# Low-rank projections ahead of the recurrence, and gemms cut in thirds, in an RWKV-7 and band-attention trunk

## The chip, the cores and the metric

The kernel runs on one core of a Trainium2 chip. The metric is the time of one execution in microseconds of device time, as the median of three runs. The engines are TensorE (PE, with its weight loads PEld), VectorE (DVE), ScalarE (ACT), GpSimd (POOL) and SyncE (SP), which issues most of the DMAs.

## The reference

One step of an encoder with a layer of RWKV-7 time mixing and a layer of chunk-band attention, each followed by a SwiGLU network, for a prompt of 1024 tokens and eight samples of 16 tokens; the width is 1024 in 16 heads of 64. The part that the change touches is the time mixing:

```python
def wkv7_scan(r, w, k, v, a, b, s0):
    def step(s, inp):
        r_t, w_t, k_t, v_t, a_t, b_t = inp
        sa = jnp.einsum('bhij,bhj->bhi', s, a_t)
        s = s * w_t[:, :, None, :] + sa[..., None] * b_t[:, :, None, :] + v_t[..., None] * k_t[:, :, None, :]
        y = jnp.einsum('bhij,bhj->bhi', s, r_t)
        return s, y
...
    r = xr @ w_r
    w_log = -jax.nn.softplus(-(w0 + jnp.tanh(xw @ w1) @ w2)) - 0.5
    decay = jnp.exp(-jnp.exp(w_log.astype(jnp.float32)))
    k = xk @ w_k
    v = xv @ w_v
    a_gate = jax.nn.sigmoid(a0 + (xa @ a1) @ a2)
    g = jax.nn.sigmoid(xg @ g1) @ g2
    kk = l2_normalize(to_heads(k * k_k, H_A))
    k = k * (1.0 + (a_gate - 1.0) * k_a)
    y, wkv_new = wkv7_scan(rh, to_heads(decay, H_A), kh, vh, -kk, kk * to_heads(a_gate, H_A), wkv_prev)
    # each head of y is normalised, scaled by ln_w, ln_b, a bonus of r, k and v is added
    out = (y * g) @ w_o
```

xr, xw, xk, xv, xa and xg are mixtures of each token's row and the row before it. The state s runs through the whole prompt; each sample has a state of its own.

## The kernel before

All tokens, 1024 of the prompt and 128 of the samples, lie in three blocks of 384. Every block goes through `proj(b)`, which computes what the recurrence reads and stores it to DRAM, in this order:

- the low-rank stage `proj_lora` (decay, gate a and output gate g), in seven steps: three inner products, two of `gates`, two of `outputs`;
- the key gemms `proj_k`, eight, one a step, each with a long tail of small operations on ScalarE and VectorE;
- the receptance gemms `proj_r`, eight, one a step, taking turns with `inverses(b)`, which forms the product of `kk` and `b` for each window (tiles `pa`, `G`, `Aab`), solves 16x16 triangles on VectorE and merges them to 64x64 inverses `TT` (tiles `t11`, `p1`);
- `proj_h` of the next block (norm and modulation), then the value gemms `proj_v`, eight, one a step.

A gemm is 24 matmuls of 128x384 into a bank `acc`: eight pieces along the width, three matmuls each, because weights and inputs are split into a high and a low part.

The recurrence is computed in windows of 128 tokens, w = 0 to 8, three a block; windows 0 to 7 are the prompt, 8 the samples. Each window has two halves of the heads, hf = 0 and 1, which run side by side. `win_prep` loads the window (tiles `XL`, `BK`, `UV`) and forms its products in banks `G`; `win_state` takes two chunks of 64 tokens, each in three steps (X, U, D, in banks `st`, two of them), and carries the state `S`; `win_y` makes the output in bank `Y`; `win_post` copies it to `y` (L1028), normalises it with two matmuls, `cen` and `var`, in banks `st`, and stores it as `yg` (L1043). A window of a block reads the values of that block, so the windows of block b run beside the projections of block b + 1:

```python
for _ in self.alternate(w, self.proj(b), 5, 4):
```

Five steps of the windows, then four of the projections, until both are done. The windows of the third block come last, in the order (6,0) (6,1) (8,0) (7,0) (7,1) (8,1), five steps to two of `early()`: first the rest of the adaLN matmuls (bank `aux`, weights `raw<-in_wada`), then the output projections of blocks 1 and 2. The third block's output projection follows when all windows are done; it reloads `yg` into tiles `mr` and splits them into `mx`.

The order in which steps are written is not the order on the engines. The framework's scheduler lays every instruction on its engine at build time, by the written order and by what it takes to be ready; each engine then runs its list in order. So the place of an instruction is read from the built program.

Of the kernel before, what the change touches and what calls it, by code (L numbers as in the profile page):

```python
# [16 lines left out]
NB = 3  # L17
TB = 384
KF = 8
KAPPA = float(np.exp(-0.5))  # L20


# [119 lines left out]
class Trunk:  # L142
# [120 lines left out]
    def gemm(self, out, W, hi, lo, m=128):  # L263

        whi, wlo = W
        for k in range(8):
            s = slice(k * m, (k + 1) * m)
            self.mm3(out, whi[:, s], wlo[:, s], hi[k], lo[k], k == 0, k == 7)


    def sq_open(self):
        return Ctx()
# [250 lines left out]
    def proj_r(self, b, hi, lo):  # L523

        nc = self.nc
        for f in range(8):
            W = self.wunit(self.pp, self.a["rw_r"][f])
            pz = self.bank("acc", 2)
            self.gemm(pz[:, :TB], W, hi, lo)
            kp = self.ev("ag", 2)  # L530
            self.load(kp, "kp", b, f)
            ex = self.ev("rr", 2)
            self.load(ex, "cs", b, f)
            nc.scalar.activation(ex, ex, AF.Exp, scale=-KAPPA)
            nc.vector.scalar_tensor_tensor(kp, pz[:, :TB], self.P("rk", f), kp, ALU.mult, ALU.mult)
            nc.vector.tensor_tensor(ex, ex, pz[:, :TB], ALU.mult)
            self.spill("r", b, f, ex)
            aux = self.bank("aux", 1)
            mm(nc, aux[:, :TB], self.C("bo"), kp, True, True)
            bn = self.ev("e0", 3)  # L540
            nc.scalar.activation(bn, aux[:, :TB], AF.Copy)
            self.save("bn", b, f, bn)
            yield
# [94 lines left out]
    def proj_v(self, b, hi, lo):  # L638

        nc = self.nc  # L640
        for f in range(8):
            W = self.wunit(self.pp, self.a["rw_v"][f])
            pz = self.bank("acc", 2)
            self.gemm(pz[:, :TB], W, hi, lo)
            if b in (2,):
                self.step(1)
            vv = self.ev("vv", 2)
            self.load(vv, "bn", b, f)
            v = self.ev("e0", 3)
            nc.scalar.activation(v, pz[:, :TB], AF.Copy)  # L650
            nc.vector.tensor_tensor(vv, vv, pz[:, :TB], ALU.mult)
            nc.scalar.activation(vv, vv, AF.Identity, bias=self.P("lnb", f))
            self.spill("v", b, f, vv)
            pt = self.bank("aux", 1)
            for w in range(3):
                nc.tensor.transpose(pt[:, w * 128:(w + 1) * 128], v[:, w * 128:(w + 1) * 128], self.C("ident"))
            vt = self.ev("e0", 3)
            nc.scalar.activation(vt, pt[:, :TB], AF.Copy)
            for e in range(2):
                nc.sync.dma_start(self.sv[b][:, :, e, f, :].rearrange("w p d -> p w d"),  # L660
                                  vt.rearrange("p (w e d) -> p e w d", w=3, e=2)[:, e])
            yield
# [7 lines left out]
    def proj_k(self, b, hi, lo):  # L670
# [3 lines left out]
        for f in range(8):  # L674
            W = self.wunit(self.pp, self.a["rw_k"][f])
            pz = self.bank("acc", 2)
            self.gemm(pz[:, :TB], W, hi, lo)
            iv = self.ev("rr", 2)
            self.load(iv, "cs", b, f)
            ag = self.ev("ag", 2)  # L680
# [337 lines left out]
    def win_post(self, w, hf, R):  # L1018

        nc = self.nc  # L1020
        b, wi = divmod(w, 3)
        fs = slice(4 * hf, 4 * hf + 4)
        gt = self.wt("gl", [128, 512], 1)
        nc.sync.dma_start(gt.rearrange("p (f t) -> p f t", f=4), self.sp[b]["g"][:, wi, fs, :])
        bv = self.wt("bv", [128, 512], 1)
        nc.sync.dma_start(bv.rearrange("p (f t) -> p f t", f=4), self.sp[b]["v"][:, wi, fs, :])
        y = self.wt("y", [128, 512], 1)
        nc.scalar.activation(y, R.Y, AF.Copy)  # L1028
        cen = self.bank("st", 2)
        mm(nc, cen, self.C("cen"), y, True, True)  # L1030
        nc.scalar.activation(y, cen, AF.Square)
        yield
        var = self.bank("st", 2)
        mm(nc, var, self.C("bo"), y, True, True)
        nc.scalar.activation(y, var, AF.Ln, bias=self.eps[:, 1:2], scale=1.0 / 64)
        nc.scalar.activation(y, y, AF.Exp, scale=-0.5)
        nc.vector.tensor_tensor(y, cen, y, ALU.mult)
        yield
        for f in range(4):
            s = slice(f * 128, (f + 1) * 128)  # L1040
            nc.vector.scalar_tensor_tensor(y[:, s], y[:, s], self.P("lnw", 4 * hf + f), bv[:, s], ALU.mult, ALU.add)
        nc.vector.tensor_tensor(y, y, gt, ALU.mult)
        nc.scalar.dma_start(self.yg[b][:, fs, wi * 128:(wi + 1) * 128], y.rearrange("p (f t) -> p f t", f=4))  # L1043
# [112 lines left out]
    def layer0a(self, ctx):  # L1156
# [4 lines left out]
        with ExitStack() as c2:  # L1161
            self.proj_open(c2)
            for _ in self.proj(0):
                pass
            for b in range(1, NB):
                w = self.windows([(w, hf) for w in range(3 * b - 3, 3 * b) for hf in range(2)])
                for _ in self.alternate(w, self.proj(b), 5, 4):
                    pass
        self.tail_open(ct)
        self.nraw, self.nhi, self.nlo = (2, 2, 2)  # L1170
# [756 lines left out]
```

## Time and profile before

| | us |
|---|---|
| median of three runs | 3878.44 (3875.95 to 3879.47) |
| profiled execution | 3879.81 |
| its span, first to last instruction | 3878.0 |
| TensorE busy | 3545.9 |
| VectorE busy | 2292.3 |
| ScalarE busy | 1570.7 |
| RWKV layer up to its last output gemm | 1334.1 |
| mean granted TensorE clock | 0.926 |

The profile is that of one execution. Busy time of TensorE is modelled from pipelined matmuls, so that a stage in which it is busy nine tenths is not yet full; the granted clock beside it says how fast it ran. A 32-bit matmul stands in the trace as two or more records, so the counts in the profile are higher than those of the program. The tables below count the program's matmuls.

### The profile page before, as it was taken

The numbers are of one execution on the slowest core, as the hardware profiler recorded it, in microseconds if no ns is written. First come the engines' busy times: TensorE is split into PE (matmuls) and PEld (weight loads), VectorE is DVE, ScalarE is ACT, GpSimd is POOL, SyncE is SP. The second block draws the span as 40 slices with busy tenths as digits, with TensorE's granted clock in tenths as the row PEclk, the third lists the DMA queues.
The fourth block names the chain that finished last, engine by engine and source line by source line (L and its number), as shares of the span: only waits on it lengthen the run. The fifth ranks groups of instructions, "written<-read, shape, count | busy, mean of one in ns | idle before, by whom it ended". The sixth has DMA issues, their size and how long they took to land.

```text
span 3878.0 us, 72281 instructions
## 1 busy us (share of the span) xinstructions
PE 3545.9 (91%) x28614; PEld 3130.7 (81%) x28614; DVE 2292.3 (59%) x4388; ACT 1570.7 (41%) x2966; POOL 570.8 (15%) x473
## 2 busy tenths in 40 slices
PE   6789889988889799999999999889889799999999
PEld 4677777867657689999887879677677799999898
DVE  4667566765435765555456842666675764555567
ACT  5555555544213533333311353465654533333310
POOL 0000000000000255444000100000000264453000
PEclk8896899798679989999999999899999899999999
DMA  5775676676646522222755113444554322222521
GB/s 205 229 237 159 182 220 170 176 219 185 185 142 194 175 71 71 75 77 77 270 192 187 68 59 100 140 141 141 150 191 162 127 79 74 74 75 92 170 84 71
DMA packets 429443, 552.31 MB, mean 142 GB/s; under 512 B 128432, under 2 KB 297520, under 8 KB 424624
## 3 DMA queue, kind: packets, MB, share of 16 engines
q1 hardware_dynamic: 374960, 528.80, 42.8%
q10 hardware_dynamic: 54144, 18.89, 2.1%
q8 instruction: 225, 3.69, 0.4%
q14 instruction: 114, 0.93, 0.1%
HBM read 413.42 MB, written 134.12 MB: 141 GB/s over the span
## 4 chain that ended last, share of the span: by engine, by line
PE 67%; DMA 11%; DVE 7%; ACT 4%; issue 2%; SPq 1%; POOL 0%; ACTq 0%; DVEq 0%; POOLq 0%
PE S L139 31%; PE PT L139 15%; PE acc L139 10%; PE st L139 3%; PE O L139 2%; PE G L139 2%; DVE h L255 1%; PE PT L1753 1%; PE Y L139 1%; PE aux L139 1%; DMA TT<-Z 1%; DMA raw<-in_wada 1%; DMA mr<-yg 1%; DMA yg<-y 1%; DMA rr<-sf_cs 1%
## 5 line engine op out<-in xcount | busy, mean ns | idle before, releaser
L139 PE MATMUL S<-h,w 128*128 128x320 f32 (+1 forms) x4944 | 696.9, 300 | 17.9 <-DVE h L255 8.3
L139 PEld LDWEIGHTS S<-h,w 128*128 128x128 f32 x4944 | 675.5, 192 | 26.0 <-DVE h L255 13.3
L139 PE MATMUL S<-h,wh 128*128 128x320 f32 (+1 forms) x2844 | 529.7, 338 | 12.7 <-DVE h L1123 6.8
L139 PE MATMUL acc<-mx,whi 128*128 128x384 f32 x1728 | 497.4, 366 | 30.3 <-ACT mx L254 12.7
L139 PEld LDWEIGHTS S<-h,wh 128*128 128x128 f32 x2844 | 455.7, 189 | 69.2 <-issue 13.3
L254 ACT ACTIVATE w<-rq 128x512 fp32r<-128x512 f32 x308 | 192.1, 629 | 502.4 <-PE S L139 199.3
L255 DVE TENSOR_TENSOR w<-rq,w 128x512 fp32r<-128x512 f32 x308 | 270.6, 882 | 199.1 <-ACT w L254 198.4
L139 PEld LDWEIGHTS acc<-mx,whi 128*128 128x128 f32 x1728 | 332.6, 201 | 60.5 <-ACT mx L254 15.6
L139 PE MATMUL PT<-h,w 128*128 128x320 f32 (+1 forms) x2448 | 355.0, 300 | 15.1 <-ACT w L254 6.9
L139 PEld LDWEIGHTS PT<-h,w 128*128 128x128 f32 x2448 | 337.4, 192 | 18.9 <-ACT w L254 7.1
L139 PE MATMUL acc<-mx,wlo 128*128 128x384 f32 x864 | 311.3, 361 | 6.6 <-DVE wlo L255 6.5
L139 PE MATMUL PT<-h,wh 128*128 128x320 f32 (+1 forms) x1428 | 287.6, 345 | 9.6 <-DVE wh L255 3.9
L1312 POOL TENSOR_TENSOR t<-t,t 128x576 f32<-128x576 f32 (+1 forms) x132 | 216.1, 1637 | 414.2 <-ACT t L1319 291.7
L139 PEld LDWEIGHTS PT<-h,wh 128*128 128x128 f32 x1428 | 234.2, 191 | 39.0 <-issue 6.9
L255 DVE TENSOR_TENSOR wlo<-raw,whi 128x1024 fp32r<-128x1024 f32 x114 | 139.9, 1230 | 96.4 <-ACT whi L254 89.3
L139 PEld LDWEIGHTS acc<-mx,wlo 128*128 128x128 f32 x864 | 172.5, 200 | 14.0 <-DVE wlo L255 9.6
L254 ACT ACTIVATE whi<-raw 128x1024 fp32r<-128x1024 f32 x114 | 119.5, 1054 | 143.0 <-PE acc L139 96.4
L255 DVE TENSOR_TENSOR h<-h,h 128x1024 fp32r<-128x1024 f32 (+4 forms) x112 | 122.9, 1112 | 84.7 <-ACT h L254 69.7
L254 ACT ACTIVATE h<-h 128x1024 fp32r<-128x1024 f32 (+4 forms) x112 | 103.2, 935 | 164.1 <-DMA h<-sd 105.3
L254 ACT ACTIVATE wh<-rq 128x512 fp32r<-128x512 f32 x124 | 74.8, 626 | 230.6 <-PE S L139 146.3
L1312 DVE TENSOR_TENSOR t<-S,t 128x576 f32<-128x576 f32 (+1 forms) x116 | 86.4, 745 | 128.5 <-PE S L139 128.5
L1379 DVE TENSOR_TENSOR h<-h,S 128x640 f32<-128x640 f32 (+1 forms) x150 | 112.1, 752 | 79.4 <-PE S L139 79.2
(423 smaller groups left out, 5712.9 us busy)
## 6 DMA issues: line engine op xcount, KB each, us to landing
h<-in_wada SPq DMA_DIRECT2D x64, 512.0 KB, 6.3
rq<-in_wg SPq DMA_DIRECT2D x88, 256.0 KB, 2.6
rq<-in_wu SPq DMA_DIRECT2D x88, 256.0 KB, 2.6
rq<-in_wd SPq DMA_DIRECT2D x88, 256.0 KB, 3.0
raw<-in_wada SPq DMA_DIRECT2D x32, 512.0 KB, 4.6
kc<-in_ck SPq DMA_DIRECT2D x16, 1024.0 KB, 5.1
vc<-in_cv SPq DMA_DIRECT2D x16, 1024.0 KB, 7.2
sd<-t SPq DMA_DIRECT2D x88, 160.0 KB, 1.9
```

What stands on the lines that cost most here:

```text
L139: return nc.tensor.matmul(out, lhsT, rhs, start=start, stop=stop)
L254: self.nc.scalar.activation(hi, x, AF.Copy)
L255: self.nc.vector.tensor_tensor(lo, x, hi, ALU.subtract)
L1312: eng.tensor_tensor(out, x, y, ALU.add)
L1379: nc.vector.tensor_tensor(y, y, d, ALU.add)
L1753: nc.tensor.transpose(pt[:, j * 128:(j + 1) * 128], P[:, j * 128:(j + 1) * 128], self.C("ident"))
```

## The change

In blocks 2 and 3 the seven low-rank steps are written ahead of the first step of the windows. Then two steps of the windows alternate with three of the projections; the key, receptance and value gemms of all blocks stop after the third and the sixth of their eight pieces, so that a gemm is three steps. The second matmul of `win_post` goes to a bank `G` in place of a bank `st`.

```diff
+LOW = 7
...
+    def gemm_steps(self, out, W, hi, lo):
+
+        whi, wlo = W
+        for k in range(8):
+            s = slice(k * 128, (k + 1) * 128)
+            self.mm3(out, whi[:, s], wlo[:, s], hi[k], lo[k], k == 0, k == 7)
+            if k in (2, 5):
+                yield
...
-            self.gemm(pz[:, :TB], W, hi, lo)
+            yield from self.gemm_steps(pz[:, :TB], W, hi, lo)
...
-        var = self.bank("st", 2)
+        var = self.bank("G", 2)
...
-                for _ in self.alternate(w, self.proj(b), 5, 4):
+                p = self.proj(b)
+                for _ in range(LOW):
+                    next(p)
+                for _ in self.alternate(w, p, 2, 3):
                     pass
```

The line with `gemm_steps` stands in `proj_k`, `proj_r` and `proj_v`.

What this does to TensorE's list is seen from its matmuls by stage. A stage runs from the first matmul of its first gemm to that of the next stage; each has 192 of its own gemms, the tail none. The tail runs from the last value gemm to the first output gemm.

| stage | before: all | windows | inverses | after: all | windows | inverses |
|---|---|---|---|---|---|---|
| block 1 low-rank | 192 | 0 | 0 | 192 | 0 | 0 |
| block 1 key | 216 | 0 | 16 | 216 | 0 | 16 |
| block 1 receptance | 247 | 0 | 48 | 247 | 0 | 48 |
| block 1 value | 439 | 0 | 224 | 439 | 0 | 224 |
| block 2 low-rank | 611 | 80 | 336 | 611 | 64 | 352 |
| block 2 key | 493 | 230 | 64 | 436 | 205 | 32 |
| block 2 receptance | 615 | 254 | 160 | 482 | 186 | 96 |
| block 2 value | 484 | 126 | 144 | 500 | 125 | 160 |
| block 3 low-rank | 611 | 96 | 320 | 577 | 158 | 224 |
| block 3 key | 471 | 223 | 48 | 479 | 88 | 192 |
| block 3 receptance | 605 | 245 | 160 | 414 | 198 | 16 |
| block 3 value | 690 | 134 | 304 | 634 | 173 | 208 |
| tail | 848 | 724 | 0 | 675 | 295 | 256 |
| output, block 1 | 371 | 179 | 0 | 470 | 278 | 0 |
| output, block 2 | 195 | 2 | 0 | 580 | 386 | 0 |
| output, block 3 | 192 | 0 | 0 | 328 | 137 | 0 |

Three places show it in the list itself. The first is TensorE in the third block's receptance stage, at the start of its third gemm (`acc_1608` before, `acc_1591` after). Before:

```order
L139 MATMUL acc_1608_9413<-mx_1346_7972,whi_1606_9409 128x384
L139 MATMUL G_1539_8944<-pa_1538_8941 64x64 x15
L139 MATMUL st_1473_8654<-xs1_1470_8632,TT_1058_6175 64x64 x8
L139 MATMUL G_1539_8944<-pa_1538_8941 64x64
L139 MATMUL Y_1545_8989<-YL_1389_8155,UV_1397_8205 64x64
L139 MATMUL G_1579_9230<-XL_1576_9220,BK_1577_9221 128x128 x3
L139 MATMUL st_1541_8965<-UV_1397_8205,BKT_1394_8184 64x64 x8
L139 MATMUL Y_1545_8989<-YL_1389_8155,UV_1397_8205 64x64 x7
L139 MATMUL Y_1545_8989<-XL_1387_8146,S0_1296_7776 64x64 x8
```

After:

```order
L140 MATMUL acc_1566_9165<-mx_1342_7834,whi_1564_9161 128x384
L140 MATMUL acc_1566_9165<-mx_1341_7833,wlo_1565_9162 128x384
L140 MATMUL G_1451_8482<-XL_1447_8471,BK_1448_8472 128x128 x4
L140 MATMUL G_1452_8495<-XL_1447_8471,BK_1448_8472 128x128 x4
L140 MATMUL aux_1551_9050<-ag_1549_9042,cst_62 128x384
L140 MATMUL acc_1591_9460<-mx_1320_7784,whi_1589_9456 128x384
L140 MATMUL acc_1591_9460<-mx_1321_7785,whi_1589_9456 128x384
L140 MATMUL acc_1591_9460<-mx_1320_7784,wlo_1590_9457 128x384
```

Before, an inverse's product (`pa`), a window's steps and its output stand inside the gemm; after, a few products of a window stand ahead of it and the gemm goes on without them.

The second place is TensorE at the end of the third block's value gemms (`acc_1794` is the last of them; `aux` from `e0` are the transposes of the values). Before, right behind the last gemm:

```order
L139 MATMUL G_1807_10994<-XL_1801_10969,BK_1802_10970 128x128
L139 MATMUL st_1824_11100<-UV_1811_11028,XL_1801_10969 64x64 x6
L656 MATMUL aux_1799_10957<-cst_62,e0_1798_10952 128x128 x3
L139 MATMUL st_1824_11100<-UV_1811_11028,XL_1801_10969 64x64 x2
L828 MATMUL G_1809_11008<-cst_62,BK_1802_10970 128x64 x8
L828 MATMUL G_1810_11009<-cst_62,BK_1802_10970 128x64 x8
L139 MATMUL G_1815_11043<-XL_1812_11033,BK_1813_11034 128x128 x4
```

After:

```order
L140 MATMUL acc_1794_10912<-mx_1525_8865,wlo_1793_10909 128x384
L140 MATMUL G_1608_9558<-XL_1603_9534,BK_1604_9535 128x128 x4
L140 MATMUL st_1628_9691<-UV_1613_9593,XL_1603_9534 64x64
L140 MATMUL G_1609_9559<-XL_1603_9534,BK_1604_9535 128x128 x4
L140 MATMUL st_1628_9691<-UV_1613_9593,XL_1603_9534 64x64 x7
L666 MATMUL aux_1799_10957<-cst_62,e0_1798_10952 128x128 x3
L838 MATMUL G_1611_9573<-cst_62,BK_1604_9535 128x64 x8
L838 MATMUL G_1612_9574<-cst_62,BK_1604_9535 128x64 x8
L140 MATMUL st_1630_9706<-xs0_1625_9677,TT_1064_6413 64x64 x8
```

Before, the window that begins there is w = 6, the first that reads these values (`UV_1811`); after, it is w = 5 (`UV_1613`, `XL_1603`), so four windows are still to go at that place in place of three.

The third place is TensorE at the last output of all windows (`Y_2047`, w = 8, hf = 1). `acc_2134` is the seventh gemm of the first block's output projection, `acc_2258` and `acc_2265` are the first two of the third block's. Before:

```order
L139 MATMUL Y_2047_12507<-XL_1967_12045,ssv_1981_12124 64x16 x11
L139 MATMUL st_2043_12477<-y_2041_12472,cst_62 128x512
L139 MATMUL Y_2047_12507<-XL_1967_12045,ssv_1981_12124 64x16 x21
L139 MATMUL acc_2134_12960<-mx_2065_12673,wlo_2133_12957 128x384
L139 MATMUL acc_2134_12960<-mx_2068_12679,whi_2132_12956 128x384
```

After:

```order
L140 MATMUL G_2043_12477<-y_2041_12472,cst_62 128x512
L140 MATMUL Y_2047_12507<-XL_1967_12045,ssv_1981_12124 64x16 x19
L140 MATMUL st_2051_12595<-y_2050_12593,cst_62 128x512
L140 MATMUL G_2052_12598<-y_2050_12593,cst_62 128x512
L140 MATMUL acc_2258_13466<-mx_2243_13436,whi_2256_13462 128x384
L140 MATMUL acc_2265_13506<-mx_2243_13436,whi_2263_13502 128x384
```

The last output moved from the first block's output projection into the third block's, past 10 gemms; in the rows after, the variance matmuls stand in banks `G`.

More of the change, by code (lines that the diff above doesn't have):

```diff
@@ L643, in proj_v @@
             pz = self.bank("acc", 2)
-            self.gemm(pz[:, :TB], W, hi, lo)
+            yield from self.gemm_steps(pz[:, :TB], W, hi, lo)
             if b in (2,):
@@ L676, in proj_k @@
             pz = self.bank("acc", 2)
-            self.gemm(pz[:, :TB], W, hi, lo)
+            yield from self.gemm_steps(pz[:, :TB], W, hi, lo)
             iv = self.ev("rr", 2)
```

## The prediction

> **What bounds the kernel now.** I read the page first: which engine carries the last chain, and at what clock.
>
> ```profile
> PE 3545.9 (91%) x28614; PEld 3130.7 (81%) x28614; DVE 2292.3 (59%) x4388; ACT 1570.7 (41%) x2966; POOL 570.8 (15%) x473
> PEclk8896899798679989999999999899999899999999
> PE 67%; DMA 11%; DVE 7%; ACT 4%; issue 2%; SPq 1%; POOL 0%; ACTq 0%; DVEq 0%; POOLq 0%
> ```
>
> The reader is to see that the chain runs two thirds of the time through TensorE, and that the granted clock (third row) has its holes in the first 14 of 40 slices, which is the RWKV layer; the rest stands at 9 and is not touched by the change. So I cut that layer into stages, each from the first matmul of one group of gemms to the first of the next, and asked for the windows: length, busy time of PE, PEld, DVE, ACT, POOL with instruction counts, granted clock, DMA share, GB/s. The first four rows are block 1 (low-rank, key, receptance, value), which has no recurrence beside it; the next eight are blocks 2 and 3; then the tail between the last value gemm and the first output gemm; then the output projection of blocks 1, 2 and 3.
>
> ```profile
> 57.90:116.10 58.20, 47.79 (x193) 38.31 (x193) 36.89 (x60) 35.76 (x63) 0.00 (x0) 0.79 0.50 162
> 116.10:178.70 62.60, 47.80 (x240) 42.24 (x240) 38.66 (x64) 33.89 (x61) 2.23 (x13) 0.85 0.80 233
> 178.70:227.70 49.00, 46.13 (x302) 40.27 (x302) 33.24 (x72) 22.47 (x39) 1.12 (x3) 0.97 0.89 282
> 227.70:295.10 67.40, 54.81 (x669) 48.68 (x666) 43.23 (x93) 39.99 (x79) 0.00 (x0) 0.87 0.65 184
> 295.10:399.60 104.50, 95.03 (x995) 77.04 (x996) 69.80 (x155) 48.77 (x91) 0.00 (x0) 0.64 0.50 146
> 399.60:481.50 81.90, 73.41 (x762) 61.37 (x761) 49.22 (x93) 45.60 (x85) 2.09 (x14) 0.91 0.65 196
> 481.50:569.40 87.90, 78.49 (x1005) 64.09 (x1004) 63.80 (x146) 46.88 (x91) 0.34 (x3) 0.93 0.76 222
> 569.40:645.10 75.70, 67.11 (x754) 58.36 (x754) 44.77 (x113) 41.48 (x82) 0.48 (x2) 0.93 0.66 187
> 645.10:735.40 90.30, 86.47 (x980) 71.52 (x979) 67.32 (x148) 49.77 (x94) 0.00 (x0) 0.71 0.58 164
> 735.40:818.00 82.60, 73.26 (x736) 60.63 (x733) 50.14 (x100) 46.55 (x96) 3.97 (x26) 0.94 0.68 197
> 818.00:908.40 90.40, 78.98 (x984) 65.10 (x984) 64.47 (x149) 43.57 (x87) 2.19 (x4) 0.93 0.76 214
> 908.40:1006.60 98.20, 90.15 (x1171) 75.17 (x1169) 47.49 (x124) 34.43 (x69) 0.00 (x0) 0.84 0.61 166
> 1006.60:1176.30 169.70, 141.87 (x1593) 100.14 (x1592) 59.62 (x151) 37.65 (x76) 0.00 (x0) 0.69 0.58 166
> 1176.30:1234.80 58.50, 58.50 (x549) 49.52 (x550) 38.11 (x76) 18.58 (x30) 0.00 (x0) 0.98 0.56 178
> 1234.80:1277.70 42.90, 39.43 (x201) 35.75 (x200) 26.48 (x41) 18.85 (x30) 0.00 (x0) 0.96 0.78 243
> 1277.70:1334.10 56.40, 41.61 (x195) 36.45 (x193) 46.71 (x86) 33.58 (x66) 19.69 (x16) 0.91 0.51 170
> ```
>
> No engine is full: TensorE is busy most of each stage, but partly at half clock, and VectorE comes to 73% at most (63.80 of 87.90). Where small matmuls stand beside dense gemms the clock is 0.91 to 0.98; where they stand alone (the tail, 0.69) or beside the short matmuls of the low-rank stage (0.64, 0.71) it falls. So it matters in which of these surroundings a small matmul stands, and the change moves them between surroundings.
>
> **The change part by part.** Nothing is computed anew: 72 gemms of blocks 1 to 3 get two stopping places each, and one bank takes another name. What moves is in the table of matmuls by stage in the section on the change; I price it against the profiled execution, 3879.8 us.
>
> Second block's low-rank stage: 611 matmuls before, 611 now, the same kinds up to 16. The recurrence cannot start there sooner or later, since it needs the inverses that block 1 finishes in that very stage. Zero.
>
> The other stages of blocks 2 and 3, up to the last value gemm: 447 fewer matmuls, nearly all out of the receptance stages (133 and 191 fewer), whose inverses and recurrence steps no longer crowd eight unbroken gemms. Price of a small matmul beside receptance gemms, second block against first: (87.90 - 49.00) / (615 - 247) = 0.106 us; beside key gemms (81.90 - 62.60) / (493 - 216) = 0.070 us. So 324 x 0.106 + 123 x 0.070 = 34.3 + 8.6: minus 43 us. At 0.070 for all it is minus 31; at the third block's receptance price, (90.40 - 49.00) / (605 - 247) = 0.116, minus 52.
>
> The tail: 848 matmuls in 169.70 us, 0.200 each, become 675, of which 256 now belong to inverses that used to run among the value gemms. All at 0.200 gives 135.1 us, minus 35. With the inverses at what they add in block 1, value against receptance stage, (67.40 - 49.00) / (439 - 247) = 0.096, it is 419 x 0.200 + 256 x 0.096 = 108.4, minus 61. No row shows inverses without gemms beside them, so I take the middle: minus 48.
>
> The output projection: the recurrence runs later, so 620 small matmuls (99, 385, 136) now stand among its 24 gemms. The first against the second of its rows gives (58.50 - 42.90) / (371 - 195) = 0.089 us, plus 55; at the receptance price plus 66. In the second block's output projection there will be two of them for each matmul of a gemm, as dense as in the receptance stage, so I take plus 60. VectorE's share there is 65% (38.11 of 58.50), which leaves room.
>
> The end: the last window now finishes inside the third block's output projection, which reads it. Before, the copy of the last result started at 1234.18, well ahead of the loads at 1276.36; now its way out lies open. The rows show the copies that start each window's end (the first half of each window, and the last half of all), the store of the last one, what a store and a reload take to land, and how long the third projection's loads kept TensorE waiting:
>
> ```profile
> 444.98 0.57 ACT L1028 ACTIVATE y<-Y 128x512 f32<-128x512 f32 x1
> 506.38 0.60 ACT L1028 ACTIVATE y<-Y 128x512 f32<-128x512 f32 x1 [1.19 <-PE Y L139]
> 595.77 0.60 ACT L1028 ACTIVATE y<-Y 128x512 f32<-128x512 f32 x1
> 775.03 0.60 ACT L1028 ACTIVATE y<-Y 128x512 f32<-128x512 f32 x1
> 844.46 0.60 ACT L1028 ACTIVATE y<-Y 128x512 f32<-128x512 f32 x1
> 931.09 0.60 ACT L1028 ACTIVATE y<-Y 128x512 f32<-128x512 f32 x1
> 1052.61 0.60 ACT L1028 ACTIVATE y<-Y 128x512 f32<-128x512 f32 x1
> 1134.19 0.60 ACT L1028 ACTIVATE y<-Y 128x512 f32<-128x512 f32 x1
> 1212.34 0.60 ACT L1028 ACTIVATE y<-Y 128x512 f32<-128x512 f32 x1 [4.12 <-PE Y L139]
> 1234.18 0.60 ACT L1028 ACTIVATE y<-Y 128x512 f32<-128x512 f32 x1 [1.24 <-DMA yg<-y]
> 1244.77 0.37 ACTq L1043 DMA_DIRECT2D yg<-y  x1
> DMA to landing us min/median/max: 2.8/3.9/5.0
> DMA to landing us min/median/max: 2.4/3.7/4.5
> 1276.36 3.77 DMA mr<-yg
> 1291.43 1.23 PE acc L139 x4
> ```
>
> Copy to store 1244.77 - 1234.18 = 10.6, landing 3.9, reload 3.7, and I add 1.2 for splitting a reloaded tile, an estimate of two operations as long as the copies above (0.60): 19.4 us with only a few gemm pieces as cover. The loads of the third projection already cost 1291.43 - 1276.36 = 15.1 in the row 1277.70. So between plus 4 (it replaces them) and plus 19 (it is added); they overlap in part, plus 10.
>
> The bank: the variance matmul of each window leaves the two banks that the recurrence steps use and takes one of those of the products before them. No instruction is added. Its cover is that a window's products are ready before the previous window ends; if that is gone, the next window's first product waits for the exponent of the last, 18 times 1.2 us at the most (two ScalarE operations of 0.60). What it saves has the same size. Zero. The queues: SP issues the same transfers, and the loads of the output projection's inputs now stand among those of the last windows, so a late window also holds those; that is in the 60.
>
> Sum: - 43 - 48 + 60 + 10 = - 21, so 3858.8 for the profiled execution; the median lies 1.4 lower, so **3857 us**. All the good ends together give - 52 - 61 + 55 + 4 = - 54, all the bad ones - 31 - 35 + 66 + 19 = + 19.
>
> **The rivals.** *The recurrence becomes the bound (slower).* At the last value gemm three windows were to go, now four, one behind the other, since each needs the state of the one before. From 1006.60 the first copy came after 46.0 us, the last half 21.8 after its first. With the pace p of a window: 46.0 + 3 p + 21.8 + 19.4 + the gemms from 1291.43 to 1334.10, 42.7, is 129.9 + 3 p; before, 327.5 passed from there to the end. With 43 us gained ahead of it the kernel is slower from p = 80.2. Paces in the rows: 61.4 and 69.4 beside key gemms, 89.4 and 86.6 beside receptance gemms, 81.6 and 78.2 in the tail. At 88 the time is 3878.4 + 129.9 + 264 - 327.5 - 43 = 3902. For it speaks that receptance gemms are most like output gemms. Against it, those two paces held the inverses of the next block, which are over by then. My sum stands for p = 73.
>
> *The surroundings don't matter.* If a small matmul costs the same everywhere, the terms up to the 60 cancel, because each matmul that leaves one stage enters another, and only the end remains: 3878 + 4 to + 19, so 3882 to 3897, or about 3878 if the freed bank pays for it. Which cause the low clock has decides this, and three more rows bear on it: two stretches at half clock, and the longest wait of TensorE in the first of those stages.
>
> ```profile
> 335.50:403.80 68.30, 61.68 (x516) 50.70 (x516) 46.46 (x107) 27.79 (x50) 0.19 (x1) 0.50 0.49 144
> 1062.60:1110.40 47.80, 42.52 (x351) 28.82 (x355) 9.89 (x23) 6.03 (x12) 0.00 (x0) 0.50 0.47 129
> PE st L139 <- issue: 2.9, 1, 2.9
> PE aux L139 <- DMA raw<-in_wada: 15.2, 9, 4.2
> ```
>
> Half clock lasted 68 us with TensorE busy 90% and no wait above 2.9 us: small matmuls alone kept it there. The fourth row leaves a door open: in the tail there are waits of up to 4.2 us for the adaLN weights, which stay.
>
> The Trainium skill (TensorE: Matmul & The Clock Gate, HAM oscillation) puts the drop to half clock down to idle gaps of TensorE of more than about 3.4 us. By that rule the tail would stay cold whatever stands in it, and the sum would be this rival's, about 3882. The 68 us row disagrees with it as the whole cause, the 4.2 us waits agree.
>
> *The clock recovers everywhere (faster still).* If small pieces between thirds of gemms keep the clock up in the tail's remainder too, its 675 matmuls cost the receptance price, 71.6 us, minus 98 in place of minus 48: 3857 - 50 = 3807. Against it: the tail still has no gemm in it.
>
> **How the numbers follow.** Two runs of this kernel can be told apart by about 0.2%, 7.8 us. My case, gains of 8 to 54 us: 0.50. Recovery: 0.08. Surroundings of no account: 0.17, most of it within 0.2%. The recurrence as bound: 0.25, from 3886 to 3915. So faster 0.58, same 0.17, slower 0.25. My case alone spans 3824 to 3870; the range reaches on to 3898, so that it leaves out recovery and the worst of the slower cases.
>
> **What would show it.** The receptance stages of blocks 2 and 3 near 74 and 70 us; the stretch from the last value gemm to the first output gemm near 122 us; the output projections of blocks 1 and 2 longer by some 50 together, at a clock above 0.9; the copies that end windows some 73 us apart from there on. The forecast is wrong if these copies stay 80 or more apart, if TensorE waits over 20 us for the last window's store, or if the output projections fall below a clock of 0.8.

## The result, and the profile after

The changed kernel takes 3923.97 us (median; 3922.2 to 3932.1), the kernel before in the same session 3877.19. The ratio is 1.0135, 95% interval 1.0115 to 1.0154: the change makes the kernel 1.35% slower, where 3857 us had been forecast.

From the page of the changed kernel: busy time of the engines, granted clock in 40 slices, the last chain by engine.

```profile
PE 3561.6 (91%) x28614; PEld 3137.7 (80%) x28614; DVE 2295.2 (59%) x4388; ACT 1581.5 (40%) x2972; POOL 574.7 (15%) x473
PEclk8886988798689789999999999899999899999999
PE 69%; DMA 12%; DVE 9%; ACT 5%; issue 2%; SPq 1%; POOL 1%; ACTq 0%; DVEq 0%; POOLq 0%
```

Nearly nothing: TensorE has 16 us more to do in a span that is 42.4 longer (3878.0 to 3920.4). Such a page can't tell where the time went, so I cut the RWKV layer at the same places as before. These are windows of the changed kernel, with the columns of before: receptance of block 2; low-rank, receptance and value of block 3; the tail; the output projections of blocks 1, 2 and 3.

```profile
469.40:544.90 75.50, 67.05 (x756) 57.15 (x756) 49.97 (x112) 34.87 (x65) 0.45 (x4) 0.95 0.77 218
...
628.00:732.90 104.90, 90.01 (x941) 71.74 (x941) 67.55 (x158) 62.95 (x107) 0.00 (x0) 0.80 0.55 160
...
805.70:874.40 68.70, 66.22 (x605) 55.26 (x604) 42.87 (x84) 36.96 (x71) 1.05 (x4) 1.00 0.77 232
874.40:977.30 102.90, 87.60 (x1041) 71.51 (x1039) 45.98 (x111) 37.86 (x75) 0.00 (x0) 0.87 0.57 161
977.30:1116.40 139.10, 100.41 (x1296) 69.88 (x1296) 55.24 (x156) 31.46 (x65) 0.00 (x0) 0.65 0.68 198
1116.40:1182.90 66.50, 66.50 (x715) 57.48 (x716) 36.84 (x70) 25.39 (x44) 0.00 (x0) 0.97 0.58 173
1182.90:1272.20 89.30, 84.00 (x937) 68.24 (x935) 53.98 (x117) 33.18 (x59) 0.00 (x0) 0.98 0.57 178
1272.20:1370.60 98.40, 68.08 (x465) 53.66 (x465) 63.38 (x129) 37.26 (x73) 20.51 (x16) 0.79 0.36 116
```

Against the rows of before: the last value gemm ends at 977.3, 29.3 us earlier than before (1006.6), and the layer at 1370.6, 36.5 later (1334.1). The tail gives 30.6 back (169.7 to 139.1), the three output projections take 96.4 more (58.5, 42.9, 56.4 became 66.5, 89.3, 98.4). So nearly all that is lost is lost behind the last value gemm: 393.3 us from there to the end of the layer, before 327.5. In that stretch TensorE is busy 319.0 us (before 281.4), and not busy 74.3 (before 46.1).

The timeline of ScalarE has the copies that end windows. These are the first halves from there on, and the last half of all:

```profile
1051.87 0.60 ACT L1038 ACTIVATE y<-Y 128x512 f32<-128x512 f32 x1
1132.62 0.60 ACT L1038 ACTIVATE y<-Y 128x512 f32<-128x512 f32 x1 [0.56 <-PE Y L140]
1199.46 0.60 ACT L1038 ACTIVATE y<-Y 128x512 f32<-128x512 f32 x1 [0.28 <-PE Y L140]
1284.30 0.60 ACT L1038 ACTIVATE y<-Y 128x512 f32<-128x512 f32 x1 [3.81 <-PE Y L140]
1303.37 0.60 ACT L1038 ACTIVATE y<-Y 128x512 f32<-128x512 f32 x1 [6.73 <-DMA yg<-y]
```

Before, three windows ended here, at 1052.61, 1134.19 and 1212.34; now four do. A window means here the two halves that run side by side; behind w = 6 these are (8,0) with (7,0), then (7,1) with (8,1). The copy at 1051.87 stands at the time of the one at 1052.61, but it belongs to w = 5, that one to w = 6. The recurrence is a whole window late, and the last copy moves from 1234.18 to 1303.37, by 69.2 us. Behind that copy lay 99.9 us before (to 1334.1) and lie 67.2 now (to 1370.6): the third output projection has come right up behind it. 69.2 less the 32.7 of slack that were there is 36.5, what the layer is longer. So at the end it is the last window and its way out that bound.

The way out, in the chain of work that led to the end of the layer (start, length, what):

```profile
1303.37 0.61 ACT y L1038
...
1312.89 2.29 DMA yg<-y
...
1361.11 1.14 DVE wlo L256
...
1362.30 8.36 PE acc L140 x46
```

The store has landed 11.8 us after the copy; the last gemm pieces come only at 1362.30, since VectorE splits the last weights (`wlo`) at 1361.11. In between it also has the next layer's splits to make: 63.38 us of its 98.40 are busy in that stage, before 46.71 of 56.40.

### The profile page after: what moved, and what is told of

It is laid out like the page before. It is cut to its first block, busy times and chain, and to the rows that moved or that the text cites. A ratio compares the mean times of both kernels' runs of the same rounds, so it can differ in the third digit from the quotient of the medians.

```text
span 3920.4 us, 72257 instructions
## 1 busy us (share of the span) xinstructions
PE 3561.6 (91%) x28614; PEld 3137.7 (80%) x28614; DVE 2295.2 (59%) x4388; ACT 1581.5 (40%) x2972; POOL 574.7 (15%) x473
## 3 DMA queue, kind: packets, MB, share of 16 engines
q1 hardware_dynamic: 374960, 528.80, 42.4%
## 4 chain that ended last, share of the span: by engine, by line
PE 69%; DMA 12%; DVE 9%; ACT 5%; issue 2%; SPq 1%; POOL 1%; ACTq 0%; DVEq 0%; POOLq 0%
PE S L140 31%; PE PT L140 15%; PE acc L140 12%; PE st L140 3%; PE G L140 2%; PE O L140 2%; DVE h L256 2%; PE PT L1766 1%; DMA yg<-y 1%; PE Y L140 1%; DMA TT<-Z 1%; PE aux L140 1%; DMA rr<-sf_cs 1%; DMA Z<-T 1%; DVE wlo L256 1%
## 5 line engine op out<-in xcount | busy, mean ns | idle before, releaser
L140 PEld LDWEIGHTS S<-h,wh 128*128 128x128 f32 x2844 | 456.4, 189 | 68.7 <-issue 13.6
L1392 DVE TENSOR_TENSOR h<-h,S 128x640 f32<-128x640 f32 (+1 forms) x150 | 111.8, 750 | 78.6 <-PE S L140 78.3
```

Of the source, the lines that this page charges most:

```text
L140: return nc.tensor.matmul(out, lhsT, rhs, start=start, stop=stop)
L1392: nc.vector.tensor_tensor(y, y, d, ALU.add)
```

## Experiments

Ratios are against the kernel before in the same session. "Half windows done" counts, in the program of TensorE, the halves of windows (18 in all) whose outputs stand ahead of the end of the last value gemm and ahead of the output projections of blocks 1, 2 and 3. The kernel before has 12, 16, 18, 18, the changed one 10, 12, 14, 16.

**The variance matmul back in its bank.** All else as in the change.

```diff
-        var = self.bank("G", 2)
+        var = self.bank("st", 2)
```

> The changed kernel with one edit undone: the variance matmul is back in a bank st. In the built program all six windows of the first two blocks end ahead of the last value gemm again, and all nine ahead of the second output projection. Theory A (the recurrence runs one window late, and the time is lost behind the last value gemm, because the variance matmul now queues for the banks of the products): 3865 us, 3845 to 3885; the stretch from the last value gemm to the last output gemm back near 325 us from 393. Theory B (the low-rank stage ahead and the pace of two to three steps make it late, the bank does nothing): 3915 to 3930. Theory C (small matmuls cost more among output gemms, wherever they come from): as A here, since they are no longer there.

Measured: 3864.79 us, ratio 0.9959 (0.9942 to 0.9975). The loss is gone and the kernel is faster than before; half windows done 12, 16, 18, 18. From the last value gemm (1000.5) to the end of the layer (1319.2) it is 318.7 us, where theory A had named some 325. The one edit that I had costed at nothing turns the sign of the result.

**The variance matmul in G, nothing else of the change.**

```diff
-        var = self.bank("st", 2)
+        var = self.bank("G", 2)
```

> The kernel before with the bank edit alone. In the built program the recurrence is late in the same way as in the changed kernel: 10, 12, 14 and 16 of the 18 half windows are done at the last value gemm and at the three output projections, against 12, 16, 18 and 18. Theory A: 3920 us, 3900 to 3940, with the loss in the output projections. Theory B: 3877, no difference.

Measured: 3909.19 us, ratio 1.0072 (1.0053 to 1.0092), half windows done 10, 12, 14, 16. The bank alone makes the recurrence a window late, and theory A's range holds. The first halves from the last value gemm (952.0) on, and the last copy:

```profile
976.26 0.60 ACT L1028 ACTIVATE y<-Y 128x512 f32<-128x512 f32 x1
1117.54 0.60 ACT L1028 ACTIVATE y<-Y 128x512 f32<-128x512 f32 x1
1185.52 0.60 ACT L1028 ACTIVATE y<-Y 128x512 f32<-128x512 f32 x1 [2.34 <-PE Y L139]
1261.30 0.60 ACT L1028 ACTIVATE y<-Y 128x512 f32<-128x512 f32 x1 [3.81 <-PE Y L139]
1283.93 0.60 ACT L1028 ACTIVATE y<-Y 128x512 f32<-128x512 f32 x1 [6.68 <-DMA yg<-y]
```

Again four windows, and the end at 1354.0, 70.1 behind the last copy. That the last value gemm came 55 us sooner than before was worth nothing.

**The change without the low-rank stage ahead.**

```diff
-LOW = 7
+LOW = 0
```

> The changed kernel without the seven low-rank steps ahead; thirds, two to three steps and the bank stay. In the built program 12, 16, 18 and 18 half windows are done at the four places. Theory A in its wide form (what counts is where the windows end, not which edit put them there): 3870 us, 3850 to 3890. Theory A in its narrow form (every kernel with the bank in G is late on the chip): 3910 or more. Theory B: 3870.

Measured: 3856.76 us, ratio 0.9945 (0.9925 to 0.9964), half windows done 12, 16, 18, 18, though the variance stays in G. A form of the bank theory by which every kernel with the variance in G is late falls here. By itself the run doesn't tell theory B from A, since both had named 3870; the two runs above do. The traces show what the low-rank stage ahead adds in the changed kernel. Timelines of the changed kernel, of this one and of the one with the bank undone, at the second window's end: the copy of its first half, the two matmuls of `win_post` (`st<-y`, then `G<-y`), the first products of the third window (`G<-XL,BK`; the products of a half are 32 records, so they can be counted off), and the copy that ends the first half of the third. Changed kernel:

```profile
515.48 0.60 ACT L1038 ACTIVATE y<-Y 128x512 f32<-128x512 f32 x1
553.61 1.02 PE L140 MATMUL st<-y,cst 128*128 128x512 f32 x2
559.13 1.02 PE L140 MATMUL G<-y,cst 128*128 128x512 f32 x2
560.70 1.16 PE L140 MATMUL G<-XL,BK 64*128 64x128 f32 x8
677.36 0.60 ACT L1038 ACTIVATE y<-Y 128x512 f32<-128x512 f32 x1
```

Without the low-rank stage ahead:

```profile
512.26 0.60 ACT L1038 ACTIVATE y<-Y 128x512 f32<-128x512 f32 x1
514.20 1.02 PE L140 MATMUL st<-y,cst 128*128 128x512 f32 x2
516.84 1.13 PE L140 MATMUL G<-y,cst 128*128 128x512 f32 x2
518.85 1.16 PE L140 MATMUL G<-XL,BK 64*128 64x128 f32 x8
610.24 0.60 ACT L1038 ACTIVATE y<-Y 128x512 f32<-128x512 f32 x1 [0.43 <-PE Y L140]
```

With the bank undone, where the products wait for no variance and come first:

```profile
491.51 0.93 PE L140 MATMUL G<-XL,BK 64*128 64x128 f32 x6
...
514.61 0.58 ACT L1038 ACTIVATE y<-Y 128x512 f32<-128x512 f32 x1
...
538.88 1.17 PE L140 MATMUL st<-y,cst 128*128 128x512 f32 x2
...
623.26 0.60 ACT L1038 ACTIVATE y<-Y 128x512 f32<-128x512 f32 x1
```

With the variance in G the products of the next window come right behind it, 1.6 and 2.0 us after its start, in both kernels that have it there. Where it comes 4.6 us after the copy, the next window starts 6.6 us after it. Where it comes 43.6 us after it, the next window starts 45.2 us after the copy, and ends 54 to 67 later than in the two others. With the bank undone `win_post` is late too, 24.3 us behind its copy, but the products don't stand behind it: they start 23.1 us ahead of the copy. So a late `win_post` holds the next window up only where the variance shares its bank. In the changed kernel TensorE isn't idle meanwhile; its costliest wait from 515 to 560 us is this one (total us, times, longest):

```profile
PE st L140 <- DVE t L882: 4.3, 4, 2.5
```

The rest of the 38 us to the first matmul of `win_post` goes to other matmuls that stand ahead of it, most of them gemms. It is the order of the list that is late, not a stall.

The same happens beside the third block's projections, in the changed kernel's timeline from 907 us (with the bank undone the same products start at 845.73, 10.3 us ahead of the copy at 856.04):

```profile
907.00 0.60 ACT L1038 ACTIVATE y<-Y 128x512 f32<-128x512 f32 x1
...
946.72 1.16 PE L140 MATMUL G<-XL,BK 64*128 64x128 f32 x8
```

This is not what makes the kernel with the bank alone late. There the second window's variance comes 5.4 us after its copy and the first three windows end within 9 us of those before; the fourth is the first late one, its products start at 721.89 (before 668.96), and the last variance ahead of them is at 634.52. What puts them there isn't shown.

**More turns for the recurrence.** The change with three steps of the windows to three of the projections.

```diff
-                for _ in self.alternate(w, p, 2, 3):
+                for _ in self.alternate(w, p, 3, 3):
```

> The changed kernel with three steps of the windows to three of the projections in place of two to three. In the built program 12, 14, 16 and 16 half windows are done at the four places: half of the lateness is made up at the last value gemm, none at the third output projection. Theory A: between the two, 3895 to 3915, with the end (waiting for the last window's store) as in the changed kernel. Theory B (pace): 3880 or less.

Measured: 3915.18 us, ratio 1.0090 (1.0062 to 1.0118), half windows done 12, 14, 16, 16. The time is at the upper edge of theory A's range, and the layer's last gemm ends 70.4 us behind the last copy (1289.65). More turns in the written order bring the windows on time at the last value gemm, but not behind it.

**Thirds alone.** The kernel before with `gemm_steps`, at a pace that has the windows about on time (12, 16, 16, 18).

```diff
-            self.gemm(pz[:, :TB], W, hi, lo)
+            yield from self.gemm_steps(pz[:, :TB], W, hi, lo)
...
-                for _ in self.alternate(w, self.proj(b), 5, 4):
+                for _ in self.alternate(w, self.proj(b), 5, 6):
```

> The kernel before with one part of the change: the gemms in thirds (and the pace at 5 half-window steps to 6 gemm steps, so that the same windows are done at the end of each block as before: 12, 16, 16, 18 half windows at the last value gemm and at the ends of the three output projections, before 12, 16, 18, 18). No low-rank stage ahead, the variance matmul stays in its old bank. Theory A (the change loses only by setting the recurrence a window late): on time here, so no loss; the receptance stages shorten by some 10 us each as in the changed kernel, and the time is 3850 to 3872. Rival B (gemms in thirds themselves cost, since small matmuls between the thirds hold each other's banks): slower than before, 3885 or more. If it stands within 0.2% of 3878, stopping places alone are worth nothing.

Measured: 3886.27 us, ratio 1.0003 (0.9988 to 1.0018): no difference, since the kernel before, run beside it, took 3886.01 us. Theory A missed, rival B's loss isn't there, and the third case holds: at this pace, stopping places alone are worth nothing. The receptance stages of blocks 2 and 3 do shorten (87.9 to 72.2, 90.4 to 78.3), and the stages behind take it back. Windows of this kernel: receptance of block 2, value of block 3, tail:

```profile
480.70:552.90 72.20, 68.23 (x670) 57.44 (x667) 42.54 (x85) 36.52 (x72) 0.45 (x4) 1.00 0.75 220
...
892.50:1003.00 110.50, 97.22 (x1210) 76.85 (x1209) 56.88 (x146) 43.22 (x87) 0.00 (x0) 0.86 0.65 188
1003.00:1184.60 181.60, 147.42 (x1975) 107.31 (x1974) 75.73 (x200) 39.17 (x82) 0.00 (x0) 0.70 0.57 164
```

The tail has 181.6 us (169.7 before), block 3's value stage 110.5 (98.2).

**Low-rank stage ahead alone.** Gemms whole, variance in st, pace 5 to 4 as before.

```diff
+                p = self.proj(b)
+                for _ in range(LOW):
+                    next(p)
-                for _ in self.alternate(w, self.proj(b), 5, 4):
+                for _ in self.alternate(w, p, 5, 4):
```

> The kernel before with the other part alone: the low-rank stages of blocks 2 and 3 ahead of the first step of the recurrence, gemms whole, old bank, pace 5 to 4 (half windows done 12, 16, 16, 18). Theory A: on time, so near the kernel before, 3865 to 3885; the low-rank stages lose their recurrence steps but these stand later beside gemms. Rival B (the low-rank stage ahead is what makes the recurrence late, whatever the bank): the first copies after the last value gemm a window late, 75 us or more apart, and 3895 to 3920.

Measured: 3862.41 us, ratio 0.9929 (0.9904 to 0.9955), half windows done 12, 16, 16, 18. On time, so the stage ahead isn't by itself what makes the recurrence late; the gain is a little above theory A's, and far from B's.

**Output projections begun in the tail.** A test of what bounds behind the last value gemm: TensorE's work, or the chain of windows. The same edit on the version without the low-rank stage ahead, and on the changed kernel. `adas()` is the loop over the adaLN steps, `outs()` the one over the two output projections.

```diff
-            for _ in range(32):
-                ...
-            for b in range(2):
-                yield from self.outproj(b)
+            yield from self.alternate(outs(), adas(), 1, 2)
```

> The fastest version so far (the change without the low-rank stage ahead, 3857) with the output projections of blocks 1 and 2 begun in the tail, one step of them to two adaLN steps, in place of behind it: 92 small matmuls stay in the tail, the rest stands among output gemms; half windows done 12, 12, 16, 18. The recurrence's own order is the same. Theory A (from the last value gemm on, the chain of windows and then the last exit set the end, 225 us to the last window's copy and some 60 behind it): TensorE's fill gains little, 3845 to 3860, the copies still 70 to 80 us apart. Rival W (TensorE's work at half clock in the tail sets it): the tail's cold stretch goes, 30 to 50 us less, 3807 to 3827.

> The changed kernel itself with the same edit: the output projections of blocks 1 and 2 begun in the tail, one step to two adaLN steps. The recurrence stays a window late (half windows done 10, 10, 12, 16). Theory A: the chain of the last four windows sets the end, so nothing is gained: 3905 to 3928, the last copy near 1300 us and the end some 67 behind it. Rival W (small matmuls and half clock on TensorE set the end): 30 us or more faster than the changed kernel, 3870 to 3895, with the last copy before 1275.

Measured: on time 3850.83 us, 0.9906 (0.9885 to 0.9926), where 0.9945 (0.9925 to 0.9964) was had without the edit. Late: 3919.24 us, 1.0085 (1.0054 to 1.0117), without it 1.0135 (1.0115 to 1.0154). The two gains are of one size, 0.4 and 0.5%, and both pairs of intervals touch. Both times lie in theory A's ranges and outside rival W's. On time two of theory A's other signs missed: the copies are 67.7 and 98.3 us apart (1038.73, 1106.46, 1204.74), and the layer ends 85.0 us behind the last copy, not some 60. Of the late one, the windows of the tail and of the third output projection, and the last copy:

```profile
978.70:996.30 17.60, 12.77 (x198) 10.02 (x198) 5.13 (x12) 7.74 (x15) 0.00 (x0) 0.81 0.76 213
...
1272.60:1373.40 100.80, 70.25 (x489) 54.18 (x489) 66.50 (x137) 39.63 (x79) 20.51 (x16) 0.76 0.37 121
```

```profile
1306.12 0.60 ACT L1038 ACTIVATE y<-Y 128x512 f32<-128x512 f32 x1 [6.52 <-DMA yg<-y]
```

The first output gemm starts 17.6 us behind the last value gemm in place of 139.1, and the layer still ends at 1373.4 (1370.6), 67.3 behind the last copy. From the last value gemm to the end it is 394.7 us against 393.3. So in the late kernel it doesn't matter where the output gemms begin; the end follows the last copy. It does so in all four late kernels, by 67.2, 67.3, 70.1 and 70.4 us, while before, with the bank undone and without the low-rank stage ahead it comes 99.9, 104.4 and 102.2 us behind it.

What the run doesn't show is what sets the time of the last copy. In both late kernels TensorE has the same 3236 records between the last value gemm and that copy, is busy 274.9 and 281.9 us of 326.1 and 327.4, and has a granted clock of 0.83 and 0.85. So the cold stretch that rival W wanted gone was mostly spread, and TensorE's work as the bound up to the last copy isn't ruled out.

**The variance in a third bank.** Is it leaving st, or sharing G?

```diff
-        var = self.bank("G", 2)
+        var = self.bank("aux", 1)
```

> The changed kernel with one word changed: the variance matmul takes the bank aux (one, shared with the sums and transposes of the projections and the adaLN matmuls), neither st as before nor G as in the change. It tells two forms of the bank's effect apart. Theory G (what makes the recurrence late is that the variance of a window holds one of the two G banks ahead of the products of the next window): on time again, half windows done 12, 18, 18, 18 at the last value gemm and at the ends... of the tail and the first two output projections, and 3845 to 3885. Rival L (leaving the st banks is what does it, wherever the variance goes): late as the change, the last window's copy near 1300 us and 3900 or more.

Measured: 3967.08 us, ratio 1.0196 (1.0164 to 1.0227), the slowest of all, with half windows done 12, 18, 18, 18. On the windows theory G was right, on the time (3845 to 3885) it missed; rival L's 3900 or more is met, but not by the late recurrence that it named. The last copy, and the windows of the receptance stages of blocks 2 and 3:

```profile
1261.73 0.60 ACT L1038 ACTIVATE y<-Y 128x512 f32<-128x512 f32 x1 [6.72 <-DMA yg<-y]
```

```profile
472.30:585.70 113.40, 99.70 (x1241) 83.17 (x1240) 66.00 (x169) 40.88 (x81) 0.74 (x4) 0.82 0.65 183
...
858.70:983.80 125.10, 103.34 (x1275) 83.88 (x1274) 70.16 (x177) 44.99 (x90) 0.38 (x2) 0.80 0.59 166
```

From the last value gemm (1107.3) to the last copy it is 154 us, less than in any other kernel, but that gemm comes 130 us later than in the change: the order went to the other extreme, with receptance stages that hold 1241 and 1275 records in place of 756 and 605. The windows aren't sooner by the clock (the sixth ends its second half at 1036.64, before at 960.41); it is the gemms that come late. So a recurrence on time isn't enough for a fast kernel. The bank aux is also used by the projections themselves (sums, transposes); whether this sharing is the cause wasn't tried by itself.

**The variance in the bank of the outputs, output projections begun in the tail.** The change with both edits; low-rank stage ahead and thirds stay.

```diff
-        var = self.bank("G", 2)
+        var = self.bank("Y", 1)
...
+            yield from self.alternate(outs(), adas(), 1, 2)
```

> The changed kernel with the variance matmul in the bank Y, and the output projections of blocks 1 and 2 begun in the tail (one step to two adaLN steps); low-rank stage ahead and thirds stay. Theory G: on time, since G is free for the next window's products; with the tail's work under output gemms the time is 3830 to 3865. Rival L: late, 3900 or more. A third way: a Y bank held for the variance delays the other half's output, and the copies of the windows lie 85 us or more apart.

Measured: 3839.93 us, ratio 0.9869 (0.9836 to 0.9901), the fastest: 1.3% below the kernel before. From the last value gemm (978.6) on:

```profile
1032.51 0.60 ACT L1038 ACTIVATE y<-Y 128x512 f32<-128x512 f32 x1
1096.00 0.60 ACT L1038 ACTIVATE y<-Y 128x512 f32<-128x512 f32 x1 [3.56 <-PE Y L140]
1171.03 0.60 ACT L1038 ACTIVATE y<-Y 128x512 f32<-128x512 f32 x1 [5.86 <-PE Y L140]
1191.92 0.60 ACT L1038 ACTIVATE y<-Y 128x512 f32<-128x512 f32 x1 [6.80 <-DMA yg<-y]
```

Its last value gemm ends within 1.3 us of the changed kernel's; three windows follow in place of four, the last copy comes 111 us sooner, the layer ends at 1291.9. At the second window's end `win_post` is as late as in the change (the copy at 500.71, its first matmul at 548.90), but the third window's products stand ahead of it, from 494.55 on. Theory G held, and the third way isn't seen: the first copies are 63.5 and 75.0 us apart. Two edits stand in this run, and how much of the 1.3% is due to each wasn't tried; begun early in four other pairs, the output projections gave 0.1 to 0.5%.

**The early output projections on two more versions.** On the low-rank stage ahead alone, and on the change with the bank undone.

> Low-rank stage ahead, gemms whole, variance in its old bank (3862 without more), with the output projections of blocks 1 and 2 begun in the tail. Here the last window's copy stands 78 us ahead of the end of the layer and its exit takes 67, so by the chain of windows no more than 11 us can be gained unless the windows themselves come closer: 3846 to 3866. If TensorE's work in the tail sets the end, 30 us or more: 3832 or less.

> The change with the variance matmul back in st (3865 without more) and the output projections of blocks 1 and 2 begun in the tail. Here the last copy stands 104 us ahead of the end and the exit takes 67, so the chain allows 37 us; the same edit on the version without the low-rank stage ahead, which had 102 us there, gave 6. Theory A: 3840 to 3862, since the small matmuls that now share TensorE with gemms make the windows later by 10 to 20 us. If the tail's work alone sets the end: 3830 or less.

Measured: 3856.99 us, 0.9920 (0.9893 to 0.9947), against 0.9929 (0.9904 to 0.9955) without it; and 3868.47 us, 0.9949 (0.9928 to 0.9969), against 0.9959 (0.9942 to 0.9975). Neither gains anything that can be measured. The first lies in its range, the second is above theory A's (3840 to 3862). There the chain left 37 us and nothing showed, so the slack behind the last copy is an upper bound of such a gain, not its size.

## Why the prediction was wrong

**The stages of blocks 2 and 3, minus 43.** Measured: from 711.5 us (295.1 to 1006.6) to 677.6 (299.7 to 977.3), minus 33.9. The receptance stages came out as said (74 and 70; measured 75.5 and 68.7). The sum was 9 us too high for the whole, since the third block's low-rank and value stages grew (90.3 to 104.9, 98.2 to 102.9). The zero for the second block's low-rank stage was minus 7.9 (104.5 to 96.6). That the size came out near says little for the prices: with the bank undone the last value gemm ends at 1000.5, 6.1 us sooner than before and not 29.3, so most of what these stages gain in the change is work put off behind them. Block 1 and what follows the layer, which I left out, are 4.6 and 5.9 longer.

**The tail, minus 48, and the output projections, plus 60 and 10.** This is the step that failed. Forecast plus 22 in all; measured minus 30.6 and plus 96.4, so plus 65.8. I summed prices of single matmuls, and such a sum doesn't say when the last window ends. Of the 65.8, TensorE is busy 37.6 and not busy 28.2, so the prices were too low and the waits were left out. In the late kernels the end follows the last copy, and starting the output gemms 121.5 us sooner (139.1 to 17.6 behind the last value gemm) doesn't bring it forward. The form that says it stood among the rivals, 129.9 + 3 p. Its terms as measured: to the first copy 74.6 (I took 46.0), three paces of 80.8, 66.8 and 84.8 (mean 77.5, I summed for 73), second half 19.1 (21.8), way out 67.2 (62.1). Together 393.3, which they must give, since they cut the stretch into pieces; my sum had stood for 349. The largest miss, 28.6, is the first copy: I had read it from before, where the last value gemm ended 29.3 us later while the window then under way ended at the same time (1052.61 and 1051.87). In the way out VectorE splits the last weights late; my own rows had it busy for 46.71 of 56.40 us in that stage, 83%, where I had read 73% as the most.

**The bank, zero.** The other failed step. I had counted and priced the fourth window behind the last value gemm, but not seen that the bank puts it there. The cover that I named, products ready before the previous window ends, is there with the bank undone (491.51 against the copy at 514.61) and is taken away by this very edit: the next products stand behind the variance in TensorE's list. And the price of the lost cover was not the two ScalarE operations, 1.2 us a window, but the place of the variance in the list: the next products start 45.2 us behind the copy in place of 23.1 ahead of it, and at 907 us 39.7 behind. Undone, the kernel is at 0.9959; alone, it costs 0.72% (0.53 to 0.92).

**The rivals.** The recurrence as bound, at 0.25, named the end that was found, but its 3886 to 3915 were too low, mostly by the first copy. Its reason, that each window needs the state of the one before, doesn't hold for the last link: (7,1) and (8,1) need no state of (8,0) and (7,0) and come behind them because the list is written so. The row of 68 us at half clock doesn't show small matmuls alone: 76 of its 516 records are 128x384 or 96x384 matmuls of the low-rank gemms, 39.8 us when their times are added up. Of the signs that I named for being wrong, copies 80 or more apart are there for two of three (80.8, 84.8); the first two output projections kept their clock (0.97 and 0.98), the third fell to 0.79; and TensorE's longest wait in the third is 9.5 us, not over 20.

**What stays open.** What sets the pace of the windows behind the last value gemm, their own steps or TensorE's other work between them: in the kernel with the variance in aux, where less stands between them, the last copies are 58.0 and 49.9 us apart. Why the bank alone makes the fourth window late. Why the scheduler sets the first matmul of `win_post` 38 us behind its copy when the low-rank stage is ahead, and 1.9 us without; that is decided when the list is built, and no trace shows it. And why the bank aux sends the order to the other extreme.

## What to carry to other kernels

Where windows that come one behind the other share an engine with dense work, count at each stage's end how many are still to go, and set a second sum beside the one by prices: windows times pace plus the way out. The pace is not fixed, since it moves with what stands between the windows (49.9 to 98.3 us in these kernels). The slack between the last window and the end (here 99.9 us, of which 67 are needed) says how late the windows may come. An edit that only renames a buffer can reorder the whole list: look at what uses that buffer next, and how late the new user stands.

## What the runs showed that I had not expected

Small matmuls can be dense and leave the clock nearly full where gemms stand beside them: in the output projection of block 2 of the changed kernel it is 0.98 with two small matmuls to each of a gemm (937 records in 89.3 us). Gemms beside them aren't enough, though: the receptance stages with the variance in aux are at 0.82 and 0.80. In the changed kernel's tail the clock is 0.65. The costliest waits of TensorE there (total us, times, longest):

```profile
PE aux L140 <- DMA raw<-in_wada: 19.8, 12, 3.2
PE G L140 <- DMA pa<-sp_b: 6.0, 2, 4.4
PE st L140 <- ACT UV L1010: 4.1, 1, 4.1
```

The Trainium skill (TensorE: Matmul & The Clock Gate, HAM oscillation) lays such a loss to idle gaps above some 3.4 us; two of these waits are longer (4.4 and 4.1), so the tail agrees with it. No run here took the waits away and left the small matmuls alone, so which of the two holds the clock down isn't settled.

A second surprise is how little a better clock brought: without the low-rank stage ahead, beginning the output projections in the tail lifted it from 0.74 to 0.83 over the first 160 to 170 us behind the last value gemm (161.2 us of tail against 169.9 with output gemms in it, so not the same work), and the kernel went from 0.9945 to 0.9906 with intervals that touch:

```profile
990.60:1151.80 161.20, 139.60 (x1576) 98.50 (x1575) 61.69 (x158) 36.92 (x75) 0.00 (x0) 0.74 0.61 176
990.00:1159.90 169.90, 150.72 (x1570) 116.78 (x1569) 80.35 (x179) 50.66 (x96) 0.00 (x0) 0.83 0.67 194
```
